# A tuned MLP kernel on one core: pinned casts at the start, and a second level of the recursion in two of the seven products of its second matmul

## The chip, the cores and the metric

One NeuronCore of a Trainium2 chip. The metric is the device time of one launch in microseconds (us), as the median of several executions.

## The reference

The kernel computes a two-layer MLP with a tanh GELU, all inputs and the output in float32.

```python
# x: (8, 1024, 1024)   w1: (1024, 4096)   w2: (4096, 1024)
def reference(x, w1, w2):
    h = x @ w1
    h = 0.5 * h * (1 + np.tanh(np.sqrt(2 / np.pi) * (h + 0.044715 * h ** 3)))
    return (h @ w2).astype(np.float32)
```

## The kernel before

The 8192 rows are worked in eight superblocks of 1024 rows, counted here from 0. In each, a first matmul (with GELU) is followed by a second matmul. Both are cut into 2 by 2 blocks and done with seven products instead of eight (a recursion in the manner of Strassen): sums and differences of blocks are made first, then seven half-size products, then their results are added with signs. Each such phase has 448 matmuls of 512 columns. Only the second matmul of superblock 0 is plain (512 matmuls), because it runs while the second weight is still being loaded, cast to fp16, and summed.

Superblock 0 also stores the cast blocks of the first weight in HBM (`raw_d`) and the summed operands of the second weight (`w2_d`). Superblock 1 reads `raw_d` back and makes the operands of the first weight (`w1_d`), and later superblocks only read. So the start of the program is full of transfers, and the rest is not.

The parts that matter here, cut; `tt` is a `tensor_tensor` on DVE (VectorE), `temp` a 128x512 fp32 tile of a pool of ten, `unit` a 4 KB-per-partition tile of a pool of 26, and `gcp` a pool of four staging tiles:

```python
def cast_in(dst, src, cast):              # fp32 weight from HBM, cast to fp16
    st = gcp.tile([P] + list(dst.shape[1:]), F32, name="gc")   # one of FOUR staging tiles
    load_in_order(st, src)                # SP queue, kept in program order
    cast(out=dst, in_=st)

def store(sb, b, q, src):
    ...
    queue = nc.gpsimd if sb < NSB - 1 else nc.sync
    return queue.dma_start(out=out2[...], in_=src)

def matmul2_first(sb, g, keep_w1):        # superblock 0, plain; b = column half of the weight
    ...
    for b in range(2):
        ...
        for q in range(NI // QC):
            raw = raw_units(QC, OH, (b + 1,))
            for j in range(0, QC, 2):
                for a in range(2):
                    cast_in(..., pool_copy if b == 0 and q < 2 else nc.scalar.copy)
            ...                           # matmuls of these rows of the weight
            if b == 0:
                if q == 0: keep_w1()
                elif q == 1: xb = x_cast(1, pool_last[0])
            else:
                ...                       # sums on DVE, written to w2_d on the SP queue
        if b == 1:
            blocks = x_transpose(xb, load_in_order)
            write(2); write(3)
        for i in range(2 * NQ):           # eight PSUM banks to evict
            ...
            if i % 2: nc.scalar.copy(out=o, in_=banks[i])
            else:     nc.vector.tensor_copy(out=o, in_=banks[i])
            last = store(sb, ..., o)

def matmul2(sb, g):                       # superblocks 1 to 7: seven products
    def product(m, banks, first):
        pieces = [load_ops(d, (m,), QC, OH)[m] for d in w2_d]
        u, v = A_TERMS[m]
        for q in range(NQ):
            if v is None: a = g[u][:, :, cols]
            else:
                a = gcp.tile([P, NI, P], GT, name="gc")
                tt(a, g[u][:, :, cols], g[v][:, :, cols], SUB)
            ...                           # 16 matmuls of 512 columns into banks[q]
            yield q, banks[q]
    ...                                   # products 4, 5, 2, 3
    for q, ps in product(1, rb, True):
        tt(d[q], d[q], ps, ADD)
    for q, ps in product(6, qb, False):
        c22 = temp(); tt(c22, d[q], ps, ADD); store(sb, "22", q, c22)
    for q, ps in product(7, rb, False):
        c11 = temp(); tt(c11, u[q], ps, ADD); last = store(sb, "11", q, c11)
    return last

for sb in range(NSB):
    g, quad = matmul1(xs, sb)
    ...                                   # second matmul
    if sb + 1 < NSB:
        xs = XOps(blocks); xs.make(5, 1, 2, 7, 6)   # five 128x2048 differences of the next x
```

## Time and profile before

| | before |
|---|---|
| time, median of 3 (range) | 1606.53 us (1605.8 to 1607.75) |
| span of the profiled execution | 1603.7 us, mean granted clock 0.996 |
| first matmul of superblock 0 | 18.3 to 130.3 us |
| second matmul of superblock 0 | 130.3 to 245.7 us |
| first matmul of superblock 1 | 245.7 to 342.6 us (96.9) |
| every later phase | 96.69 us |
| last matmul starts / span ends | 1599.4 / 1603.7 us |

Such phase times are read from the trace: a phase runs from the start of its first matmul to the start of the first matmul of the next phase.

Three lines of the page of the kernel before: the span, PE's busy time with its share of the span, and the chain that ended last, by engine.

```profile
span 1603.7 us, 18985 instructions
...
PE 1578.2 (98%) x7296; PEld 717.9 (45%) x7296; DVE 819.6 (51%) x1047; ACT 472.3 (29%) x784; POOL 132.1 (8%) x228
...
PE 95%; DMA 3%; DVE 1%; ACT 1%; issue 0%; SPq 0%; POOL 0%; DVEq 0%
...
```

PE (TensorE) is the limit. The chain of the kernel before, followed in time (start, length, what, how many), shows how regular it is after the start:

```profile
...
245.89 96.87 PE ps L277 x448
342.76 96.69 PE ps L461 x448
...
```

448 matmuls in 96.69 us are 215.8 ns each, with no wait at all. Time can only be saved there by streaming fewer columns. The start is different. The waits of PE of the kernel before (total us, times, longest):

```profile
...
PE ps L277 <- ACT g_216 L287: 7.7, 2, 7.4
...
PE ps L395 <- DVE tmp L443: 3.3, 1, 3.3
...
```

So PE stands once for 7.4 us behind a GELU, which itself stands behind casts on ACT (ScalarE), and once for 3.3 us behind a PSUM eviction on DVE. Both are holes in the start. The cast in front of that GELU was itself waiting for its weight, as the ACT queue of the kernel before shows (start, length, what, and in brackets the idle time before and what ended it):

```profile
...
118.76 1.04 ACT L137 CAST u<-gc 128x1024 f16<-128x1024 f32 x1 [8.00 <-DMA gc<-in_w_dram]
...
```

So the first hole comes from a transfer that is late. Three stretches of the kernel before, of which two are in the start and one reaches into superblock 1 (from and to, length, busy us and instructions of PE, weight load, DVE, ACT, POOL, then the clock, the DMA share, and GB/s):

```profile
...
105.00:115.00 10.00, 10.00 (x49) 4.52 (x47) 4.20 (x7) 5.43 (x8) 2.58 (x6) 1.00 1.04 265
115.00:124.00 9.00, 1.59 (x6) 0.53 (x5) 1.28 (x2) 4.44 (x7) 0.00 (x0) 0.75 0.97 307
232.00:247.00 15.00, 15.00 (x71) 6.76 (x70) 3.84 (x5) 2.55 (x5) 4.42 (x9) 1.00 0.89 349
...
```

In the first two stretches the DMA engines are full (1.04 and 0.97; a share can come out a little over 1), though PE has only 1.59 us of work in the second. In the third PE is busy throughout. The third view of the kernel before is its SP queue, which issues loads and stores in program order (start, time from first to last issue, what, how many):

```profile
...
89.33 44.96 SPq L115 DMA_DIRECT2D gc<-in_w_dram  x20
...
160.05 26.67 SPq L115 DMA_TRANSPOSE u<-xb  x16
...
202.99 4.79 SPq L152 DMA_DIRECT2D u<-raw_d_81  x4
...
```

These are 20 loads of the second weight into the staging tiles, the sixteen transposing loads of the next x, and the first loads of `raw_d` for superblock 1.

### The profile page before, as it was taken

What the parts mean: (1) busy time and instruction counts of PE and PEld (TensorE: products, weight loads), DVE (VectorE), ACT (ScalarE), POOL (GpSimd) and SP (SyncE); (2) the same over time, 40 slices, a digit from 0 to 9 for tenths busy, and PEclk for the clock granted to TensorE, in tenths of its full rate; (3) what the DMA queues carried; (4) which work ended last, traced back from release to release, by engine and by line L of the source; (5) the groups of instructions that cost most, each with busy time, mean ns of one, the idle gap of its engine ahead of it and who ended that gap; (6) DMA issues with size and microseconds to landing.
All of it is one profiled execution on the core that took longest, in us unless ns stands there. A gap on an engine that the chain in (4) does not pass through costs nothing.

```text
span 1603.7 us, 18985 instructions
## 1 busy us (share of the span) xinstructions
PE 1578.2 (98%) x7296; PEld 717.9 (45%) x7296; DVE 819.6 (51%) x1047; ACT 472.3 (29%) x784; POOL 132.1 (8%) x228
## 2 busy tenths in 40 slices
PE   7989999999999999999999999999999999999999
PEld 4434444444444444444444444444444444444444
DVE  6855336644455444555445554456534555455433
ACT  4645104431044210441114410244103431044310
POOL 2230113001100012000120000100001000000000
PEclk9999999999999999999999999999999999999999
DMA  9999998674566646546574565746557464544511
GB/s 306 345 316 361 276 397 280 179 288 146 197 188 184 236 171 228 157 153 262 186 221 144 169 238 197 227 131 226 201 203 246 102 265 158 210 157 178 216 53 53
DMA packets 161820, 338.91 MB, mean 211 GB/s; under 512 B 72257, under 2 KB 78401, under 8 KB 160833
## 3 DMA queue, kind: packets, MB, share of 16 engines
q1 hardware_dynamic: 146944, 278.97, 50.4%
q0 software_dynamic: 14784, 58.73, 11.5%
q8 instruction: 57, 0.93, 0.2%
q14 instruction: 35, 0.28, 0.1%
HBM read 266.34 MB, written 85.98 MB: 220 GB/s over the span
## 4 chain that ended last, share of the span: by engine, by line
PE 95%; DMA 3%; DVE 1%; ACT 1%; issue 0%; SPq 0%; POOL 0%; DVEq 0%
PE ps L277 46%; PE ps L461 42%; PE ps L395 7%; DMA gc<-in_w_dram 2%; DVE u L107 1%; ACT u L137 0%; DVE tmp L107 0%; DMA u<-in_x_dram 0%; DMA u<-xb 0%; SPq L115 0%; POOL u L118 0%; ACT g_218 L287 0%; ACT g_216 L287 0%; ACT g_217 L287 0%; ACT tmp L343 0%
## 5 line engine op out<-in xcount | busy, mean ns | idle before, releaser
L277 PE MATMUL ps<-u 128*128 128x512 f16 x3584 | 779.8, 380 | 13.1 <-ACT g_216 L287 7.7
L107 DVE TENSOR_TENSOR tmp<-tmp,ps 128x512 f32<-128x512 f32 x652 | 447.1, 687 | 661.6 <-PE ps L461 333.3
L277 PEld LDWEIGHTS <-u 128*128 128x128 f16 x3584 | 351.1, 98 | 440.3 <-issue 15.9
L461 PE MATMUL ps<-u,gc 128*128 128x512 f16 x2240 | 485.7, 379 | 0.0
L461 PEld LDWEIGHTS <-gc 128*128 128x128 bf16 x2240 | 219.2, 98 | 264.3
L375 POOL DMA_DIRECT2D out_dram<-tmp x112 | 60.6, 542 | 1108.0 <-ACT tmp L481 733.9
L107 DVE TENSOR_TENSOR u<-u 128x2048 f16<-128x2048 f16 (+2 forms) x110 | 123.0, 1152 | 56.6 <-ACT u L137 21.5
L343 ACT COPY tmp<-ps 128x512 f32<-128x512 f32 x128 | 73.0, 570 | 258.2 <-PE ps L277 258.2
L107 DVE TENSOR_TENSOR tmp<-ps,tmp 128x512 f32<-128x512 f32 x128 | 88.4, 691 | 5.9 <-PE ps L277 1.2
L481 ACT COPY tmp<-ps 128x512 f32<-128x512 f32 x28 | 16.4, 586 | 177.3 <-PE ps L461 177.3
L395 PE MATMUL ps<-u,g_217 128*128 128x512 f16 x128 | 49.0, 383 | 3.3 <-DVE tmp L443 3.3
L395 PE MATMUL ps<-u,g_218 128*128 128x512 f16 x128 | 49.0, 383 | 0.0
L395 PE MATMUL ps<-u,g_215 128*128 128x512 f16 x128 | 48.9, 382 | 0.0
L395 PE MATMUL ps<-u,g_216 128*128 128x512 f16 x128 | 48.8, 381 | 0.0
L137 ACT CAST u<-gc 128x1024 f16<-128x1024 f32 x36 | 37.2, 1044 | 37.6 <-DMA gc<-in_w_dram 37.6
L487 ACT COPY tmp<-ps 128x512 f32<-128x512 f32 x28 | 16.4, 586 | 80.3 <-PE ps L461 80.3
L475 ACT COPY tmp<-ps 128x512 f32<-128x512 f32 x28 | 16.4, 586 | 74.9 <-PE ps L461 74.9
L118 POOL CAST u<-gc 128x1024 f16<-128x1024 f32 (+1 forms) x26 | 28.5, 1105 | 73.8 <-DMA gc<-in_w_dram 60.0
L254 POOL DMA_DIRECT2D xb<-in_x_dram x56 | 27.5, 509 | 18.1 <-DMA out_dram<-tmp 14.5
L441 ACT COPY tmp<-ps 128x512 f32<-128x512 f32 x8 | 4.7, 586 | 71.1 <-PE ps L395 71.1
L395 PEld LDWEIGHTS <-g_218 128*128 128x128 bf16 x128 | 12.6, 98 | 18.8 <-issue 3.9
L395 PEld LDWEIGHTS <-g_215 128*128 128x128 bf16 x128 | 12.6, 99 | 15.5 <-issue 0.8
(120 smaller groups left out, 848.8 us busy)
## 6 DMA issues: line engine op xcount, KB each, us to landing
gc<-in_w_dram SPq DMA_DIRECT2D x64, 512.0 KB, 6.8
out_dram<-tmp POOLq DMA_DIRECT2D x112, 256.0 KB, 4.4
u<-w_d_85 SPq DMA_DIRECT2D x49, 512.0 KB, 6.4
u<-w_d_86 SPq DMA_DIRECT2D x49, 512.0 KB, 7.1
u<-w_d_87 SPq DMA_DIRECT2D x49, 512.0 KB, 5.8
u<-w_d_88 SPq DMA_DIRECT2D x49, 512.0 KB, 6.3
u<-w_d_77 SPq DMA_DIRECT2D x42, 512.0 KB, 4.8
u<-w_d_78 SPq DMA_DIRECT2D x42, 512.0 KB, 5.1
```

What stands on the lines that cost most here:

```text
L107: nc.vector.tensor_tensor(out=out, in0=in0, in1=in1, op=op)
L118: pool_last[0] = nc.gpsimd.tensor_copy(out=out, in_=in_)
L137: cast(out=dst, in_=st)
L254: nc.gpsimd.dma_start(out=xb[q:q + P, :], in_=x2[s * SB + q:s * SB + q + P, :])
L277: nc.tensor.matmul(bank, lhsT=ops[m][:, k, cs], rhs=xs[m][:, k, :], start=(first and k == 0), stop=(k == KH - 1), skip_group_check=not first,)
L343: nc.scalar.copy(out=v, in_=pb)
L375: return queue.dma_start(out=out2[r0:r0 + P, o0:o0 + OH], in_=src)
L395: nc.tensor.matmul(banks[i], lhsT=g[f"{i // NQ + 1}{a + 1}"][:, c, (i % NQ) * P:(i % NQ + 1) * P], rhs=w[a], start=(c == 0 and a == 0), st ...
L461: nc.tensor.matmul(banks[q], lhsT=a[:, c, :], rhs=pieces[c // QC][:, c % QC, :], start=(first and c == 0), stop=(c == NI - 1), skip_group_ ...
L475: nc.scalar.copy(out=v[q], in_=ps)
L481: nc.scalar.copy(out=c21, in_=ps)
L487: nc.scalar.copy(out=c12, in_=ps)
```

## The change

It has three parts. At the start, the casts of the second weight that ACT does are pinned behind the last GELU of the first matmul, some of them go to POOL (GpSimd), and the PSUM evictions go to ACT, to close both holes. From superblock 2 on, products 6 and 7 of the second matmul get a second level of the recursion: instead of 64 matmuls of 512 columns each takes seven small products of 16 matmuls of 256 columns, so 112 x 256 columns in place of 128 x 256, an eighth less. For this superblock 1 splits the operands of these products into `in_d`, and the sums that products 6 and 7 are added to, which were temporaries, become tiles of the pool of 26. And GELU's output is fp16 instead of bf16.

```diff
-GT = mybir.dt.bfloat16
+GT = mybir.dt.float16
+INNER = (6, 7)
+ORDER = (4, 5, 1, 2, 3, 7, 6)
 ...
+    def act_late_copy(out, in_):
+        with tc.issue_after(gelu_last[0].ins):
+            nc.scalar.copy(out=out, in_=in_)
 ...
-            nc.scalar.activation(out=g[b][:, c, :], in_=src, func=GELU)
+            gelu_last[0] = nc.scalar.activation(out=g[b][:, c, :], in_=src, func=GELU)
 ...                                      # matmul2_first
-                            pool_copy if b == 0 and q < 2 else nc.scalar.copy,
+                            pool_copy if (q == 0 if b == 0 else j) else act_late_copy,
 ...
-                    elif q == 1:
+                    elif q == 3:
                         xb = x_cast(1, pool_last[0])
 ...
-                if i % 2:
-                    nc.scalar.copy(out=o, in_=banks[i])
-                else:
-                    nc.vector.tensor_copy(out=o, in_=banks[i])
+                nc.scalar.copy(out=o, in_=banks[i])
 ...
+    def inner_product(m, g, acc):
+        ...                               # seven loads of in_d on the SP queue
+        def outer(b):                     # a block of the product's left operand, made once
+            ...
+                tt(x[b], g[u0][at], g[v0][at], SUB)
+        def product(j, bank, first):
+            u, v = A_TERMS[j]
+            if v is None: t = outer(u)
+            else:
+                p, q = outer(u), outer(v)
+                t = gcp.tile([P, HK, HT // 2], GT, name="gc")
+                tt(t, p, q, SUB)
+            ...                           # 16 matmuls of 256 columns
+        product(4, pb, True)
+        v = temp(); nc.scalar.copy(out=v, in_=pb)
+        product(5, qb, True)
+        u = temp(); tt(u, v, qb, SUB)
+        nc.gpsimd.tensor_tensor(out=part("11"), in0=part("11"), in1=pair(u), op=ADD)
+        ...                               # products 1, 2, 3, 7, 6; one more add on gpsimd
 ...                                      # matmul2
         for q, ps in product(1, rb, True):
             tt(d[q], d[q], ps, ADD)
-        ...                               # products 6 and 7 as above
+            if sb > 1:
+                tt(u[q], u[q], ps, ADD)
+        for m, b, acc2, acc, banks in ((6, "22", d2, d, qb), (7, "11", u2, u, rb)):
+            if sb > 1:
+                inner_product(m, g, acc2)
+                for q in range(NQ):
+                    last = store(sb, b, q, acc[q])
+            else:
+                ...                       # as before
```

More of the change, by code (lines that the diff above doesn't have):

```diff
@@ L94 @@
     raw_d = [dram.tile([P, 4, KH * QW], DT, name=f"raw_d{q}") for q in range(NI // QC)]
+    in_d = {m: dram.tile([P, 7, NI // 2, OH // 2], DT, name=f"in_d{m}") for m in INNER}
     w2_d = [dram.tile([P, 7, QC * OH], DT, name=f"w2_d{q}") for q in range(NI // QC)]
@@ L132, in make_sum @@
         tt(ops[m][:, :, sl], raw[u][:, :, sl], raw[v][:, :, sl], op)
+    def act_late_copy(out, in_):
+        with tc.issue_after(gelu_last[0].ins):
+            nc.scalar.copy(out=out, in_=in_)
+    gelu_last = [None]
     def cast_in(dst, src, cast):
@@ L304, in ahead @@
                 if step == 0:
-                    quads.append(load_ops(w1_d[q], (4, 5, 1, 2, 3, 7, 6), KH, QW))
+                    quads.append(load_ops(w1_d[q], ORDER, KH, QW))
                 return
@@ L439, in matmul2_first, with split_inner, block @@
                 o = temp()
-                if i % 2:
-                    nc.scalar.copy(out=o, in_=banks[i])
-                else:
-                    nc.vector.tensor_copy(out=o, in_=banks[i])
+                nc.scalar.copy(out=o, in_=banks[i])
                 last = store(sb, f"{i // NQ + 1}{b + 1}", i % NQ, o)
         return last, blocks
+    def split_inner(m, pieces):
+        def block(k, b, h):
+            return pieces[2 * k + h][:, :, b * OH // 2:(b + 1) * OH // 2]
+        for j in ORDER:
+            u, op, v = B_TERMS[j]
+            d = in_d[m][:, j - 1]
+            t = None if op is None else unit(NI // 2, OH // 2)
+            for h in range(2):
+                cs = slice(h * QC, (h + 1) * QC)
+                x0 = block(int(u[0]) - 1, int(u[1]) - 1, h)
+                if op is None:
+                    nc.gpsimd.dma_start(out=d[:, cs, :], in_=x0)
+                else:
+                    tt(t[:, cs, :], x0, block(int(v[0]) - 1, int(v[1]) - 1, h), op)
+            if op is not None:
+                nc.gpsimd.dma_start(out=d, in_=t)
@@ new lines, in inner_product, with part, pair @@
+    def inner_product(m, g, acc):
+        HK, HO = NI // 2, OH // 2
+        u0, v0 = A_TERMS[m]
+        x = {}
+        y = {}
+        for j in ORDER:
+            y[j] = unit(HK, HO)
+            nc.sync.dma_start(out=y[j], in_=in_d[m][:, j - 1])
+        def outer(b):
+            if b not in x:
+                a, k = int(b[0]) - 1, int(b[1]) - 1
+                x[b] = unit(HK, HT // 2)
+                at = (slice(None), slice(k * HK, (k + 1) * HK), slice(a * HT // 2, (a + 1) * HT // 2))
+                tt(x[b], g[u0][at], g[v0][at], SUB)
+            return x[b]
+        def product(j, bank, first):
+            u, v = A_TERMS[j]
+            if v is None:
+                t = outer(u)
+            else:
+                p, q = outer(u), outer(v)
+                t = gcp.tile([P, HK, HT // 2], GT, name="gc")
+                tt(t, p, q, SUB)
+            for i in range(2):
+                for c in range(HK):
+                    nc.tensor.matmul(
+                        bank[:, i * HO:(i + 1) * HO],
+                        lhsT=t[:, c, i * P:(i + 1) * P],
+                        rhs=y[j][:, c, :],
+                        start=(first and i == 0 and c == 0),
+                        stop=(c == HK - 1),
+                        skip_group_check=not first or i > 0,
+                    )
+        def part(b):
+            a, o = int(b[0]) - 1, int(b[1]) - 1
+            return acc[a][:, :, o * HO:(o + 1) * HO]
+        def pair(t):
+            return t.rearrange("p (i n) -> p i n", i=2)
+        pb, qb, rb = psum(), psum(), psum()
+        product(4, pb, True)
+        v = temp()
+        nc.scalar.copy(out=v, in_=pb)
+        product(5, qb, True)
+        u = temp()
+        tt(u, v, qb, SUB)
+        nc.gpsimd.tensor_tensor(out=part("11"), in0=part("11"), in1=pair(u), op=ADD)
+        product(1, rb, True)
+        s = temp()
+        tt(s, u, rb, ADD)
+        product(2, pb, False)
+        s2 = temp()
+        tt(s2, s, pb, SUB)
+        nc.gpsimd.tensor_tensor(out=part("22"), in0=part("22"), in1=pair(s2), op=ADD)
+        tt(part("21"), part("21"), pair(pb), ADD)
+        product(3, qb, False)
+        tt(part("12"), part("12"), pair(qb), ADD)
+        product(7, rb, False)
+        tt(part("11"), part("11"), pair(rb), ADD)
+        product(6, qb, False)
+        tt(part("22"), part("22"), pair(qb), ADD)
@@ L469, in product, with halves @@
                 yield q, banks[q]
-        v, u, d, s2 = {}, {}, {}, {}
+            if m in INNER:
+                split_inner(m, pieces)
+        def halves():
+            tiles = [up.tile([P, 2, OH], F32, name="u") for _ in range(2)]
+            return tiles, [tiles[q // 2][:, q % 2, :] for q in range(NQ)]
+        v = {}
         pb, qb, rb = [], [], []
@@ L475, in matmul2 @@
             nc.scalar.copy(out=v[q], in_=ps)
+        u2, u = halves()
         for q, ps in product(5, qb, True):
-            u[q] = temp()
             tt(u[q], v[q], ps, SUB)
+        d2, d = halves()
         for q, ps in product(2, pb, False):
@@ L482, in matmul2 @@
             store(sb, "21", q, c21)
-            d[q] = temp()
             tt(d[q], u[q], ps, SUB)
@@ L488, in matmul2 @@
             store(sb, "12", q, c12)
+            if sb > 1:
+                tt(d[q], d[q], ps, ADD)
         for q, ps in product(1, rb, True):
             tt(d[q], d[q], ps, ADD)
-        for q, ps in product(6, qb, False):
-            c22 = temp()
-            tt(c22, d[q], ps, ADD)
-            store(sb, "22", q, c22)
-        for q, ps in product(7, rb, False):
-            c11 = temp()
-            tt(c11, u[q], ps, ADD)
-            last = store(sb, "11", q, c11)
+            if sb > 1:
+                tt(u[q], u[q], ps, ADD)
+        for m, b, acc2, acc, banks in ((6, "22", d2, d, qb), (7, "11", u2, u, rb)):
+            if sb > 1:
+                inner_product(m, g, acc2)
+                for q in range(NQ):
+                    last = store(sb, b, q, acc[q])
+            else:
+                for q, ps in product(m, banks, False):
+                    c = temp()
+                    tt(c, acc[q], ps, ADD)
+                    last = store(sb, b, q, c)
         return last
```

## The prediction

> **What bounds the kernel now.** TensorE: the page gives PE 98% of the 1603.7 us span, and 95% of the chain that ended last. In order of time that chain shows, from 246 us on, phases (first, then second matmul of superblocks 1 to 7) of 448 matmuls in about 96.7 us each unbroken: 215.8 ns per 512-column matmul, clock 1.00. There only fewer columns can save. The start has two holes, by windows: from 104.6 to 130 us 76 matmuls start (16.4 us of work in 25.4), and from 188 to 196 us 17 (3.7 in 8). Timeline: weight casts ahead of GELUs on ACT wait 8 us for a DMA; a PSUM eviction on DVE sits behind a sum that waits 7.2 us for x transposes. About 13 us are recoverable. DMA is 95% or more busy there, which limits it.
>
> **What the change does.**
> 1. Casts of the second weight are pinned behind the last GELU and shared with POOL; evictions go to ACT. Both holes should close: estimate 11 us. The b=1 casts had 20 us of slack, so they stay hidden.
> 2. In superblocks 2 to 7, products 6 and 7 go from 64 matmuls of 512 columns (13.81 us) to 112 of 256. The Trainium skill's "TensorE: Matmul & The Clock Gate", section "Back-to-back issue gap", gives N/2.4 + 2.5 ns; the trace agrees at 512. At 256 that is 109 ns (estimate), 12.23 us a product: 1.58 us saved, 12 times: 19 us at most. Unshown: that a weight load (98 ns in the groups) hides at 256.
> 3. DVE pays. Before, a product needs 4 subtractions of 128x2048 (1.22 us, 1.15 back to back) and 4 PSUM adds (0.69, 0.62). An inner product needs 9 subtractions and 7 PSUM ops, besides 2 adds on POOL. From product 1 to the end of product 7 DVE has about 40 us of work against 38 of PE. PE runs product 6 nearly free, then waits in product 7 for operands: I estimate 1.3 us per superblock, 2.5 with the POOL adds ("SBUF — State Buffer": the shared port pair is an exclusive lock between GpSimd and DVE ops with two SBUF inputs; not shown by this trace). So 3.16 us saved less 2.5 lost, six times: 4 us net.
> 4. Superblock 1 splits two weights: 20 half-size sums on DVE, 7.3 MB of writes, once: 1 us lost. Operand reads rise by 3.1 MB per later superblock, on 212 GB/s: hidden.
> 5. GELU in fp16: no time.
>
> **Sum.** 1606.5 - 11 - 4 + 1 = 1592 us; 8 in 10: 1579 to 1606. Chances: faster over 2% 0.05, within 2% 0.93, slower 0.02.
>
> **What would show it.** Step 1: superblock 1 starts near 233 us instead of 246; on ACT no cast of the second weight before the last GELU. Step 2: 1344 matmuls of 256 columns, spaced 109 ns where fed. Step 3: PE waits on DVE operands, 1 to 4 us per superblock, in product 7; DVE above 90% busy in the last 38 us of each second matmul, which takes about 96 us. Step 4: phases of superblock 1 within 2 us of 96.7.
>
> **What would make it wrong.** Weight loads not hidden at 256 columns (each 10 ns costs 13 us); POOL adds that block DVE longer, or late weights at the next superblock's start: slower. DVE ahead of my layout: up to 15 us faster. DMA saturation keeping the holes: 10 us slower.

## More of the kernel before

Last, DVE of the kernel before, the first sums of superblock 1 (start, length, what, how many, and in brackets the idle time before and what ended it):

```profile
...
213.41 7.09 DVE L107 TENSOR_TENSOR u<-u 128x2048 f16<-128x2048 f16 x6 [17.25 <-DMA u<-raw_d_81]
...
```

They start 32 us before superblock 1 needs them (213.4 against 245.7).

## The result, and the profile after

The changed kernel took 1621.9 us (median of 4, 1620.85 to 1623.54) against 1607.14 us (1605.8 to 1608.67) for the kernel before on the same chip. The ratio is 1.0092, with a 95% interval of 1.0075 to 1.011. Ratios here and below are the mean time of one kernel's fast runs over that of the other's of the same rounds, so not quite the ratio of the medians. The prediction of 1592 us, with a range up to 1606, was wrong: the change costs 0.9% where a gain of 0.9% was predicted.

| phase, us | before | after | what it adds to the span |
|---|---|---|---|
| first matmul of superblock 1 starts | 245.7 | 232.2 | -13.5 |
| first matmul of superblock 1 | 96.87 | 116.39 | +19.5 |
| second of 1, first of 2 | 96.69 each | 96.69 each | 0 |
| second matmul of superblocks 2 to 6 | 96.69 | 95.52 (69.07 + 26.45) | 5 x -1.17 |
| first matmul that follows it (3 to 7) | 96.69 | 98.21 | 5 x +1.52 |
| second matmul of superblock 7, to the start of the last matmul | 96.5 | 102.0 | +5.5 |
| from the start of the last matmul to the end | 4.4 | 7.1 | +2.7 |

The entries sum to 15.95 us, and the two spans differ by 16.0. 69.07 us are products 4, 5, 2, 3 and 1, which the change leaves alone, and 26.45 us are the two products that it splits (27.62 before).

The page of the kernel after, the same three lines:

```profile
span 1619.7 us, 20521 instructions
...
PE 1568.4 (97%) x7872; PEld 774.0 (48%) x7872; DVE 947.9 (59%) x1203; ACT 481.0 (30%) x800; POOL 188.6 (12%) x274
...
PE 1%; DVE 1%; issue 0%; DVEq 0%
...
```

The chain that ended last now has about 1% of the span in it: it is followed back only over the last part of superblock 7, and is of no use for the rest. The waits of PE of the kernel after answer better:

```profile
...
PE ps L288 <- DVE tmp L111: 21.8, 11, 8.6
PE ps L503 <- DVE gc L111: 8.0, 6, 3.2
...
PE ps L556 <- DMA u<-w_d_87: 2.1, 1, 2.1
...
PE ps L556 <- DMA u<-w_d_90: 0.7, 1, 0.7
...
```

The two holes of the start are gone from the list. In their place PE waits 21.8 us in first matmuls (line 288) for temporaries of DVE, 14.4 of them in superblock 1, 8.0 us in the small products (line 503) for differences of DVE, and 2.8 us in superblock 7 for weight loads. The same stretches of the kernel after:

```profile
...
105.00:115.00 10.00, 10.00 (x48) 4.53 (x47) 6.00 (x9) 4.75 (x8) 0.00 (x0) 1.00 0.56 167
115.00:124.00 9.00, 9.00 (x43) 4.05 (x42) 5.47 (x8) 5.41 (x9) 0.00 (x0) 1.00 0.00 1
232.00:247.00 15.00, 6.17 (x23) 2.45 (x24) 11.55 (x12) 2.34 (x4) 5.89 (x11) 0.74 1.02 395
...
```

From 105 to 124 us PE is now busy throughout, as intended. But the DMA share falls to 0.56 and then to 0.00. And at the start of superblock 1 PE has 6.17 us of work in 15, at a mean clock of 0.74, while the DMA engines are full (1.02, before 0.89). The SP queue of the kernel after, the same three groups:

```profile
...
89.73 58.08 SPq L119 DMA_DIRECT2D gc<-in_w_dram  x20
...
175.74 30.70 SPq L119 DMA_TRANSPOSE u<-xb  x16
...
222.46 3.74 SPq L163 DMA_DIRECT2D u<-raw_d_81  x4
...
```

The 20 weight loads take until 147.8 us instead of 134.3, and all that stands behind them in the queue is later: the transposes by 15.7 us, the loads of `raw_d` by 19.5 us. DVE of the kernel after, at the start of superblock 1:

```profile
...
230.91 2.47 DVE L111 TENSOR_TENSOR u<-u 128x2048 f16<-128x2048 f16 x2 [17.00 <-DMA u<-raw_d_81]
...
245.72 0.69 DVE L111 TENSOR_TENSOR tmp<-tmp,ps 128x512 f32<-128x512 f32 x1 [0.18 <-DMA out_dram<-tmp]
...
250.85 0.69 DVE L111 TENSOR_TENSOR tmp<-tmp,ps 128x512 f32<-128x512 f32 x1 [2.70 <-DMA out_dram<-tmp]
...
```

The first sums of superblock 1 begin at 230.9 us, 17.5 us later than before, and 1.3 us before PE begins the phase. Then DVE waits for stores (`out_dram<-tmp`) to give temporaries back.

Now the second level. Two products of superblock 2 in the kernel before and in the kernel after, by the same stretch (columns as above):

```profile
...
609.00:635.00 26.00, 26.00 (x122) 11.80 (x121) 10.14 (x13) 0.59 (x1) 4.91 (x10) 1.00 0.54 191
...
```

```profile
...
609.00:635.00 26.00, 24.56 (x213) 20.47 (x211) 25.00 (x29) 1.17 (x2) 8.09 (x8) 1.00 0.62 210
...
```

DVE goes from 10.14 us busy to 25.00 of 26. PE of the kernel after in the same place of superblock 3, with its waits in brackets:

```profile
...
813.54 1.91 PE L503 MATMUL ps<-u,gc 128*128 128x256 f16 x16
815.77 1.91 PE L503 MATMUL ps<-u,gc 128*128 128x256 f16 x16 [0.31 <-DVE u L111]
...
820.37 3.67 PE L503 MATMUL ps<-u,gc 128*128 128x256 f16 x32 [0.95 <-DVE gc L111]
...
```

Where PE is fed, small matmuls start 109 ns apart: the 32 of the last line take 3.67 us, the drain of the last one included. In front of them it waits (0.31 and 0.95 us in the brackets) for `u` and `gc`, the operands that DVE makes. The additions on POOL, from the groups of the kernel after (count, busy us, mean ns of one, idle time before and what ended it):

```profile
...
L526 POOL TENSOR_TENSOR u<-u,tmp 128x512 f32<-128x512 f32 x12 | 26.1, 2172 | 279.4 <-DMA u<-in_d_86 223.1 <-DVE tmp L111 56.2
...
L533 POOL TENSOR_TENSOR u<-u,tmp 128x512 f32<-128x512 f32 x12 | 15.2, 1264 | 24.4 <-DVE tmp L111 18.5 <-DMA u<-w_d_77 5.9
...
```

The same addition of 128x512 elements takes 2172 ns in the first place and 1264 in the second; e6 comes back to this.

### The profile page after: what moved, and what is told of

Read it like the earlier page. It is cut to its first block, busy times and chain, and to the rows that moved or that the text cites. A ratio compares the mean times of both kernels' runs of the same rounds, so it can differ in the third digit from the quotient of the medians.

```text
span 1619.7 us, 20521 instructions
## 1 busy us (share of the span) xinstructions
PE 1568.4 (97%) x7872; PEld 774.0 (48%) x7872; DVE 947.9 (59%) x1203; ACT 481.0 (30%) x800; POOL 188.6 (12%) x274
## 5 line engine op out<-in xcount | busy, mean ns | idle before, releaser
L288 PE MATMUL ps<-u 128*128 128x512 f16 x3584 | 785.2, 381 | 26.2 <-DVE tmp L111 21.8
L111 DVE TENSOR_TENSOR tmp<-tmp,ps 128x512 f32<-128x512 f32 x548 | 375.0, 686 | 287.9 <-ACT tmp L354 116.1
L556 PE MATMUL ps<-u,gc 128*128 128x512 f16 x1472 | 320.0, 379 | 0.0
L556 PEld LDWEIGHTS <-gc 128*128 128x128 f16 x1472 | 143.9, 98 | 173.8
L111 DVE TENSOR_TENSOR u<-u,ps 128x512 f32<-128x512 f32 x152 | 101.1, 681 | 98.4 <-ACT tmp L588 66.3
L386 POOL DMA_DIRECT2D out_dram<-tmp x72 | 39.1, 544 | 815.5 <-ACT tmp L583 723.5
L503 PE MATMUL ps<-u,gc 128*128 128x256 f16 x960 | 112.8, 275 | 10.4 <-DVE gc L111 8.0
L354 ACT COPY tmp<-ps 128x512 f32<-128x512 f32 x128 | 73.0, 571 | 117.1 <-PE ps L288 117.1
L503 PEld LDWEIGHTS <-gc 128*128 128x128 f16 x960 | 93.7, 99 | 26.5 <-DVE gc L111 11.6
L111 DVE TENSOR_TENSOR u<-tmp,ps 128x512 f32<-128x512 f32 x28 | 19.3, 688 | 119.0 <-PE ps L556 95.6
L111 DVE TENSOR_TENSOR gc<-u 128x2048 f16<-128x2048 f16 x60 | 74.1, 1267 | 0.0
L583 ACT COPY tmp<-ps 128x512 f32<-128x512 f32 x28 | 16.4, 586 | 177.3 <-PE ps L556 177.3
L526 POOL TENSOR_TENSOR u<-u,tmp 128x512 f32<-128x512 f32 x12 | 26.1, 2172 | 279.4 <-DMA u<-in_d_86 223.1
L522 ACT COPY tmp<-ps 128x512 f32<-128x512 f32 x12 | 7.0, 586 | 162.8 <-PE ps L503 162.8
```

What stands on the lines that cost most here:

```text
L111: nc.vector.tensor_tensor(out=out, in0=in0, in1=in1, op=op)
L288: nc.tensor.matmul(bank, lhsT=ops[m][:, k, cs], rhs=xs[m][:, k, :], start=(first and k == 0), stop=(k == KH - 1), skip_group_check=not first,)
L354: nc.scalar.copy(out=v, in_=pb)
L386: return queue.dma_start(out=out2[r0:r0 + P, o0:o0 + OH], in_=src)
L503: nc.tensor.matmul(bank[:, i * HO:(i + 1) * HO], lhsT=t[:, c, i * P:(i + 1) * P], rhs=y[j][:, c, :], start=(first and i == 0 and c == 0), ...
L522: nc.scalar.copy(out=v, in_=pb)
```

## The experiments

Seventeen kernels ran. All gave the right result except two that were wrong, as said there. This table holds what was measured; "m2" is the second matmul of superblocks 2 to 6 (its two products 6 and 7 alone in brackets), "next m1" the first matmul behind it.

| run | time, us | ratio [95%] | first matmul of superblock 1: start, length | m2 | next m1 |
|---|---|---|---|---|---|
| after | 1621.9 | 1.0092 [1.0075, 1.011] | 232.2, 116.4 | 95.52 (26.45) | 98.21 |
| e1 | 1612.26 | 1.003 [1.0015, 1.0045] | 231.3, 116.5 | 96.69 | 96.69 |
| e3 | 1608.19 | 1.0006 [0.999, 1.0023] | 241.8, 98.3 | 96.69 | 96.69 |
| e4 | 1605.53 | 0.9989 [0.9968, 1.0009] | 232.0, 113.8 | 96.69 | 96.69 |
| e8 | 1608.77 | 1.0012 [0.9997, 1.0027] | 244.4, 102.5 | 96.69 | 96.69 |
| e13 (wrong) | 1594.36 | 0.9924 [0.991, 0.9937] | 234.3, 100.9 | 96.69 | 96.69 |
| e2 | 1618.35 | 1.0068 [1.0052, 1.0083] | 249.9, 97.3 | 95.52 (26.45) | 98.2 |
| e5 (wrong) | 1596.0 | 0.9935 [0.992, 0.995] | 245.4, 97.5 | 93.8 (24.75, once 25.10) | 96.69, once 98.86 |
| e6 | 1616.79 | 1.0064 [1.0048, 1.0079] | 246.2, 97.5 | 96.2 (27.09) | 98.1 |
| e7 | 1606.67 | 1.0003 [0.9986, 1.002] | 244.3, 96.9 | 95.84 (12.96 + 13.81) | 96.69 |
| e11 | 1606.33 | 0.9994 [0.998, 1.0008] | 247.0, 96.9 | 96.69 | 96.69 |
| e9 | 1617.82 | 1.0068 [1.0055, 1.0082] | 245.1, 97.8 | 95.5 (26.45) | 98.2 |
| e10 | 1695.09 | 1.0547 [1.0531, 1.0563] | 248.4, 110.4 | 95.51 (26.45) | 110 to 112 |
| e14 | 1629.18 | 1.0139 [1.0124, 1.0154] | 247.3, 97.4 | 99.0 to 100.2 (29.9 to 31.1) | 96.69 |
| e15 | 1624.56 | 1.0109 [1.0096, 1.0122] | 241.6, 100.6 | 99.0 to 100.1 (29.9 to 31.05) | 96.69 |
| e12 | 1607.4 | 1.0005 [0.9993, 1.0018] | 243.1, 100.0 | 95.84 (12.96 + 13.81) | 96.69 |
| e16 | 1601.87 | 0.9969 [0.9956, 0.9982] | 241.8, 100.7 | 95.84 (12.97 + 13.81) | 96.69 |
| e17 | 1608.69 | 1.0009 [0.9996, 1.0023] | 242.6, 103.1 | 95.07 (26.00, once 26.35) | 96.69 |

The time of the kernel before in these batches was 1606.19 to 1607.74 us. A start of the same instructions varies by some us between executions: superblock 1 begins at 245.7 us in the kernel before and at 249.9 us in e2, which has the same start. So differences of a few us in that column are not read. Behind the first matmul of superblock 1 the phases of e1, e3, e4, e8 and e13 have the same lengths in all traces, so for these five the total times compare the end of that matmul over all executions, and not only in the profiled one.

### The start: e1, e3, e4, e8, e13

My first theory was that the pin starves the DMA engines: casts that wait for the last GELU hold all four staging tiles, so that no weight is loaded meanwhile. The rivals were the second level's extra traffic and the moved evictions.

**e1: the start of the change alone**, on the kernel before.

```diff
 # the kernel before, with act_late_copy and gelu_last as in the change, and
-  pool_copy if b == 0 and q < 2 else nc.scalar.copy,
+  pool_copy if (q == 0 if b == 0 else j) else act_late_copy,
-  elif q == 1:
+  elif q == 3:
       xb = x_cast(1, pool_last[0])
-  if i % 2: nc.scalar.copy(out=o, in_=banks[i])
-  else:     nc.vector.tensor_copy(out=o, in_=banks[i])
+  nc.scalar.copy(out=o, in_=banks[i])
```

> The kernel before with only the changed start: second-weight casts pinned behind the last GELU and shared with POOL, all evictions on ACT, x cast issued at the fourth quarter. Theory A (the start as a whole loses: pinned casts hold the four staging tiles, the SP queue stops issuing loads, every later load is 13 to 18 us later and the next superblock's first matmul waits): superblock 1 starts near 232 us but its first matmul takes about 115 us, total about 6 us slower than before, 1613 us. Rival B (the start gains its 13 us; the loss in superblock 1 comes from the other parts, more rows in the pools and the split of the weights): first matmul of superblock 1 takes 97 us, total 1593 us.

Superblock 1 starts at 231.3 us and its first matmul takes 116.5 us, as in the kernel after. Everything later is 96.69 us. So the loss in superblock 1 belongs to the start, and the second level has no part in it. Stretches of e1:

```profile
...
105.00:115.00 10.00, 10.00 (x48) 4.52 (x47) 5.79 (x9) 4.94 (x9) 0.00 (x0) 1.00 0.46 143
115.00:124.00 9.00, 9.00 (x43) 4.08 (x42) 5.26 (x7) 5.65 (x9) 0.00 (x0) 1.00 0.00 1
...
```

**e3: e1 without the pin.**

```diff
-  pool_copy if (q == 0 if b == 0 else j) else act_late_copy,
+  pool_copy if (q == 0 if b == 0 else j) else nc.scalar.copy,
```

> e1 without the pin alone: casts on the same engines, but where the scheduler puts them. Theory A: loads are issued between 98 and 124 us again, superblock 1's first matmul falls from about 115 to about 97 us, while the hole in front of the last GELUs comes back (about 9 us); eviction on ACT keeps its 4 us: total about 1602 us. Rival C (not the pin but the POOL casts behind output stores, or the earlier x cast, delay the loads): the first matmul of superblock 1 stays above 110 us.

The DMA engines stay busy, the first hole is back, and superblock 1 is no longer slow (98.3 us). The profiled execution is e3's fastest (1602.93 us; the others took 1607.65 to 1608.84), but the other kernels without the pin, e12 and e15 to e17, agree with 100.0 to 103.1 us. Stretches of e3:

```profile
...
105.00:115.00 10.00, 4.80 (x15) 1.84 (x15) 2.69 (x5) 6.56 (x9) 0.00 (x0) 0.83 0.83 266
115.00:124.00 9.00, 8.94 (x42) 3.82 (x41) 4.55 (x8) 8.80 (x14) 0.00 (x0) 1.00 0.96 312
...
```

PE has 13.74 us of work in these 19, against 19.00 in e1, and DMA 0.83 and 0.96 instead of 0.46 and 0.00. The time is that of the kernel before (1.0006). So the pin does both: it closes the hole and starves the transfers. Up to 124 us the rates and lengths of two stretches (0 to 124 and 124 to 232 us, not printed) give 35.7 MB moved with the pin (288 GB/s times 124 us, in e1 and after), 39.7 MB in e3, and 40.2 MB before. At 232 us it is 69.3 MB after and 76.8 MB before.

**e4: POOL does all casts of the first half** and ACT only few of the second.

```diff
-  pool_copy if (q == 0 if b == 0 else j) else act_late_copy,
+  pool_copy if (b == 0 or j) else act_late_copy,
```

> e1 with all casts of the first half of the second weight on POOL, which waits for no GELU; the pin stays for the second half. Theory A: staging tiles come free at once, no DMA hole at 105 to 124 us, superblock 1 starts near 232 us and its first matmul takes 97 to 102 us: total 1593 to 1598 us. Rival D (DMA bandwidth itself bounds the start, whatever the order): the first matmul of superblock 1 ends no earlier than in before, 342 us, total 1605 us or more.

Now nothing waits for GELU in the first half, the transfers keep up (40.1 MB at 124 us), and the hole is closed: superblock 1 begins at 232.0 us. Yet its first matmul takes 113.8 us, and it ends at 345.8, no earlier than before (342.6). So starvation is not the whole story: over all executions e4, which has none, is 6.6 us faster than e1 (means), and yet no faster than the kernel before (0.9989 [0.9968, 1.0009]). The profiled execution is e4's slowest (1608.68 us; the others took 1602.4 to 1606.4), so its end at 345.8 is some us later than usual. The trace of e4 shows two waits there, 5.1 us behind sums that wait for a `raw_d` load, and 8.0 us for temporaries held by stores. Between 232 and 262 us its DMA share is 1.03 and 1.05 (shown below, beside e13).

**e8: e4 with the output stores of superblock 0 on ACT's queue.**

```diff
-  queue = nc.gpsimd if sb < NSB - 1 else nc.sync
+  queue = nc.scalar if sb == 0 else nc.gpsimd if sb < NSB - 1 else nc.sync
```

> e4 with superblock 0's output stores issued from the ACT queue instead of POOL's, where they stand behind weight stores that wait for DMA. If the 8.5 us stall at 242 us (DVE waits for a free temporary, that is for such a store) is POOL's queue order: it goes, superblock 1's first matmul falls from 113.8 to about 105 us, total 1597 us. Rival D (DMA is saturated there, so the wait only moves): it stays above 110 us.

This missed. ACT evicts PSUM and now also waits to issue stores, so that PE waits 7.6 us for evictions in the second matmul of superblock 0, and superblock 1 begins at 244.4 us. Its first matmul is shorter (102.5 us) but ends at 346.8, much as in e4 (345.8). Moving the wait to another queue does not remove it.

**e13: e4 with 6.3 MB less to write.** Three of the four writes of `raw_d` are left out and all loads read the one that is written, so the result is wrong; the bytes read stay the same.

```diff
-  for b, t in self.raw.items():
+  for b, t in self.raw.items() if self.q == 0 else ():        # keep_raw
-  nc.sync.dma_start(out=flat(t), in_=raw_d[q][...])
+  nc.sync.dma_start(out=flat(t), in_=raw_d[0][...])
```

> e4 with three of the four raw copies of the first weight not written (superblock 1 reads the first copy four times; result wrong on purpose): 6.3 MB less DMA before 140 us, nothing else. In e4 the PE hole is closed and yet superblock 1's first matmul ends at 345.8 us. Theory D (from 124 us the start is bound by DMA throughput of about 400 GB/s): loads run earlier by up to 16 us, superblock 1's first matmul falls from 113.8 to 97 to 104 us and ends at 329 to 337 us; total 1590 to 1598 us. Rival I (bytes do not matter, the order of queues does): it ends after 342 us again.

The first matmul of superblock 1 takes 100.9 us instead of 113.8, and ends at 335.2 us, 10.6 us earlier than in e4. Stretches of e4, then of e13:

```profile
...
232.00:247.00 15.00, 5.47 (x21) 2.12 (x20) 1.88 (x3) 2.37 (x4) 4.82 (x9) 0.71 1.03 419
247.00:262.00 15.00, 11.38 (x43) 4.64 (x43) 5.61 (x9) 4.14 (x7) 6.61 (x13) 0.72 1.05 315
...
```

```profile
...
232.00:247.00 15.00, 11.10 (x53) 4.93 (x51) 5.36 (x7) 4.57 (x8) 8.99 (x18) 1.00 1.01 356
247.00:262.00 15.00, 15.00 (x71) 6.77 (x70) 10.85 (x15) 7.46 (x13) 1.73 (x4) 1.00 0.77 187
...
```

In e4 the DMA engines are full in both, and PE has 5.47 and 11.38 us of work in 15. In e13 the share is down to 0.77 in the second, and PE is busy there. So fewer bytes make superblock 1 earlier, where closing the holes did not: at full DMA, an earlier first use does not make data come earlier, and closing the holes alone moves the wait to superblock 1. One rival stays open: e13 takes the twelve writes out of the SP queue too, and superblock 1 no longer waits for them before it reads, so bytes and queue are not told apart. That another queue did not help in e8 fits the Trainium skill, "DMA: Bandwidth & Descriptors", section "Issuing engines are not separate DMA queues", which says that transfers of all issuing engines end up on the same 16 DMA engines; the full share in e4, with stores on one queue and loads on another, is in line with it.

### The second level: e2, e5, e6, e7, e11

**e2: the second level alone**, with the start of the kernel before.

```diff
 # the kernel after, with
-  pool_copy if (q == 0 if b == 0 else j) else act_late_copy,
+  pool_copy if b == 0 and q < 2 else nc.scalar.copy,
-  elif q == 3:
+  elif q == 1:
       xb = x_cast(1, pool_last[0])
-  nc.scalar.copy(out=o, in_=banks[i])
+  if i % 2: nc.scalar.copy(out=o, in_=banks[i])
+  else:     nc.vector.tensor_copy(out=o, in_=banks[i])
```

> The changed kernel with the start of before (casts, evictions, x cast as before). Theory A: the second level costs about 10 us by itself (0.35 us in each of superblocks 2 to 6, 5.4 us in superblock 7, 2.9 us in the tail), so about 1617 us, and the first matmul of superblock 1 takes 97 us. Rival B: that matmul still takes over 110 us and the total is above 1625 us.

It costs 0.7% by itself. Its phases repeat those of the kernel after: 26.45 us instead of 27.62, then 98.2 instead of 96.69, superblock 7 at 101.7, and 7.0 us after the last matmul.

**e5: e2 without the inner differences** (wrong): the small products use a block itself.

```diff
-  p, q = outer(u), outer(v)
-  t = gcp.tile([P, HK, HT // 2], GT, name="gc")
-  tt(t, p, q, SUB)
+  t = outer(u)
+  outer(v)
```

> e2 with the five operand subtractions of each small product left out (result wrong on purpose; all matmuls, loads and PSUM work stay): 11.5 us of DVE work less per second matmul. Theory A (DVE's queue is what PE waits for): the fourteen small products take 24.5 us instead of 26.45, the next first matmul 96.7 instead of 98.2, superblock 7's small products about 24.5 instead of 29.8; total about 1600 us. Rival E (256-column matmuls or the operand loads are the limit): the small products stay at 26 us or more.

The two products take 24.75 us, and the next first matmul 96.69 (in one superblock each, 25.10 and 98.86). Stretches of e5, from the start of two split products to the end of the next first matmul:

```profile
...
799.00:826.00 27.00, 26.51 (x232) 22.36 (x230) 20.94 (x26) 1.76 (x3) 11.70 (x14) 1.00 0.66 239
826.00:923.00 97.00, 97.00 (x451) 44.01 (x450) 56.56 (x82) 46.35 (x79) 3.42 (x8) 1.00 0.70 234
...
```

224 matmuls at 109.2 ns are 24.46 us (worked out), so weight loads do hide at 256 columns, and 2.87 of the 3.16 us per superblock are gained (27.62 before) when DVE has five differences less to make per product. The formula in the Trainium skill, "TensorE: Matmul & The Clock Gate", section "Back-to-back issue gap" (109 ns at 256), holds. So what superblocks 2 to 6 lose is lost to DVE's five differences per product. Two losses stay in e5: products 4, 5, 2, 3 and 1 of superblock 7 still take 72.95 us instead of 69.07, and the end still takes 7.0 us (both are taken up under e9).

**e6: e2 with the two additions per product moved from POOL to DVE.**

```diff
-  nc.gpsimd.tensor_tensor(out=part("11"), in0=part("11"), in1=pair(u), op=ADD)
+  tt(part("11"), part("11"), pair(u), ADD)
   # and the same for part("22")
```

> e2 with the four POOL adds per superblock on DVE. Theory A with a small lock: DVE gets 2.4 us more and loses about 2 us of lock waits, so small products 26 to 27.5 us, next first matmul 98 to 99 us, total within 8 us of e2. Rival F (the POOL adds, which take 2.2 us and stretch DVE subtractions to 1.7 us and more, are the main loss): small products fall below 25.5 us and the total by 6 us or more.

27.09 and 98.1 us, against 26.45 and 98.2 in e2. The wait of PE for differences grows from 8.0 us in e2 to this in e6:

```profile
...
PE ps L506 <- DVE gc L111: 13.2, 11, 3.2
...
```

The POOL additions and DVE's differences do hold each other up. In superblock 3 of the kernel after, an addition that starts 0.17 us into a difference takes 2.17 us instead of 1.26, and a difference that starts 0.43 us into an addition takes 1.92 us instead of 1.22. So whichever starts first keeps the other waiting. This agrees with the exclusive lock described in the Trainium skill, "SBUF — State Buffer", section "SBUF: two separate sides", which the trace of the kernel before could not show. But the same additions done on DVE cost as much, so moving them gains nothing in the products; what the lock costs by itself was not measured. The end does change: 4.9 us pass after the last matmul, against 7.0 in e2 (see e9).

**e7: only product 6 at the second level.**

```diff
-INNER = (6, 7)
+INNER = (6,)
   # and without the addition of product 1 to u
```

> e2 with the second level in product 6 alone, product 7 as before. Theory A: DVE has a whole normal product to catch up, so product 6 costs 12.3 to 12.7 us, the next first matmul 96.7: superblocks 2 to 7 gain 1.1 to 1.5 us each; total 1600 to 1606 us, 12 to 18 below e2. If the second level loses in itself, whatever DVE does, it is half of e2's loss: about 1612 us.

Product 6 takes 12.96 us (12.23 would be without waits, 13.81 before), product 7 its 13.81, and the next first matmul 96.69: a gain of 0.85 us in each of five superblocks. Superblock 7 gives it back (100.5 us; PE waits for weight loads behind stores), and the time is that of before, 1.0003.

**e11: fp16 for GELU's output alone.**

```diff
-GT = mybir.dt.bfloat16
+GT = mybir.dt.float16
```

> The kernel before with GELU's output in fp16 alone. All theories: within 3 us of before (the start varies by that), every phase after superblock 0 at 96.69 us, weight load 98 ns, GELU 630 and 597 ns.

All phases take 96.69 us and the ratio is 0.9994. It costs nothing.

### Where things stand in the queues: e9, e10, e14, e15

**e9: e2 with all stores on POOL's queue**, in the last superblock too.

```diff
-  queue = nc.gpsimd if sb < NSB - 1 else nc.sync
+  queue = nc.gpsimd
```

> e2 with the last superblock's output stores on POOL's queue like all others, instead of SP's. Theory A for superblock 7 (stores that wait for results stand in SP's queue ahead of weight loads; and the scheduler, having other queues to fill, orders DVE there unlike elsewhere): its second matmul takes 95.5 us as in superblocks 2 to 6 instead of 101.7, total 4 to 7 us below e2's 1618. Rival G (superblock 7 is slow because no next x and weights are loaded, so something else is late): it stays at 100 us or more.

The second matmul of superblock 7 falls from 101.7 us to 95.4 (69.07 + 26.34), like the others. So its loss came from stores that stood ahead of weight loads in the SP queue, which also changed the order in which the scheduler (which orders each engine's queue when the program is built) put DVE's work. But the end is lost again: the last stores of e9 on POOL are issued here, and the span ends at 1613.9 us.

```profile
...
1601.67 1.07 POOL L386 DMA_DIRECT2D out_dram<-u  x2 [0.76 <-DVE u L111]
```

From the last matmul to the end it takes 13.6 us, against 7.0 in e2. The total does not move.

It is not the landing of these stores that takes so long: their last packet is there at 1604.5 us. What ends last is a `DRAIN` that closes POOL's queue. Its groups in e9, in the kernel after, and in e16 (below), in this order (line, queue, how many; shortest, median and longest in ns; first and last start):

```profile
...
L651 POOLq DRAIN  x3: 46/93/11010, 1602.1 to 1613.6; - x3
...
```

```profile
...
L648 POOLq DRAIN  x3: 46/102/10377, 1608.5 to 1619.4; - x3
...
```

```profile
...
L646 POOLq DRAIN  x3: 46/93/8646, 1582.5 to 1598.3; - x3
...
```

The first and longest of them starts with POOL's last instruction and takes 11.0 us in e9, 10.4 us in the kernel after. In all nine traces with about 7 us or more after the last matmul (after, e2, e5, e9, e10, e12, e14, e15, e17) the span ends 0.8 us after it, and it ends 8.3 to 10.4 us after POOL's last instruction. In the other ten (4.2 to 4.9 us) POOL was done early and the `DRAIN` was over before the last stores landed, as in e16, where it ends at 1591.2 us. So the end of these nine hangs on when POOL gets its last instruction, be it a store (e9, e12) or one of the second level's additions (the other seven). Why it takes so long, no run shows.

**e10: e2 with the five x differences made ahead of the second matmul.** In e2 they stand in DVE's queue at the start of the next first matmul.

```diff
+  xs = XOps(blocks); xs.make(5, 1, 2, 7, 6)     # moved ahead of
   last = matmul2(sb, g)
```

> e2 with the five sums of the next superblock's x written ahead of the second matmul instead of after it, so that they do not stand in DVE's queue between the last small product and the next first matmul. Theory A: the first matmuls of superblocks 3 to 7 fall from 98.2 to about 96.8 us, the small products stay near 26.4; total 6 to 8 us below e2. Rival H (the first matmul is late for its weights): 98.2 us stays.

This missed badly: the first matmuls of superblocks 1 to 6 take 110 to 112 us. In the DVE queue the differences now stand ahead of work of the first matmul, and wait up to 14.0 us for transposes; behind the longer waits the matmuls also start 427 instead of 216 ns apart for some us. Waits of PE of e10:

```profile
...
PE ps L288 <- DVE tmp L111: 60.7, 9, 12.3
...
```

(The rows of this view are total, times, longest.) Superblock 7 has no next x, and its first matmul takes 96.69 us. That the x differences cause the 1.5 us is thereby made likely; e14 shows it.

**e14: e2 with the x differences between products 3 and 1.**

```diff
   for q, ps in product(3, qb, False):
       ...
+  xs = XOps(blocks); xs.make(5, 1, 2, 7, 6)
   for q, ps in product(1, rb, True):
```

> e2 with the five sums of the next x between products 3 and 1, where DVE has room and the x blocks have landed (e10 put them too early, in front of the transposes). Theory A: first matmuls of superblocks 3 to 7 take 96.7 us instead of 98.2; small products 26 to 27 us; total 6 to 8 us below e2. If the first matmul waits for something else, 98.2 stays.

The next first matmul is 96.69 us in every superblock: the 1.5 us were the x differences. But the two products grow from 26.45 to 29.9 or more. Waits of PE of e14:

```profile
...
PE ps L506 <- DVE gc L111: 19.3, 6, 3.2
...
```

The scheduler now puts all four blocks of product 7 ahead of its first difference, and PE waits 3.2 us once per superblock. It is the order that superblock 7 has in the kernel after and in e2.

**e15: the kernel after without the pin, with the x differences as in e14, and with a changed queue for stores.**

```diff
+  pool_copy if (q == 0 if b == 0 else j) else nc.scalar.copy,
+  queue = nc.gpsimd if sb < NSB - 1 or b != "11" else nc.sync
   # and e14's edit
```

> A version meant to beat both kernels: changed kernel without the pin, x sums as in e14, the last superblock's stores on POOL except its last product's on SP (e9's tail was 13.6 us with all on POOL). Second matmuls 95.5, first ones 96.7, start as before or 3 us better, tail about 6 us: 1597 to 1602 us.

This missed: it is the same as e14, first matmuls at 96.69, products at 29.9 to 31.05. In superblock 7 they take 26.34, as in e9, since most stores are off the SP queue.

**e17: both products, with DVE's order from product 1 to product 7 laid down by hand.** The operands of product 6 are made during product 1, and those of product 7 between the additions of product 6.

```diff
+  def ptt(out, in0, in1, op):
+      tc.keep_in_program_order(nc.vector.tensor_tensor(out=out, in0=in0, in1=in1, op=op))
   # used for all DVE work of these products, in an order written out; else as e15
```

> Both products at the second level, first casts not pinned, x sums made between products 3 and 1 as in e14 and e15, but the order of the vector engine's queue from product 1 to product 7 is laid down by hand: operands of product 6 are made during product 1, those of product 7 between product 6's additions, and no operand stands behind another that waits. My theory (the small products lose to the order of the vector queue, not to the matmuls): small products 24.5 to 25.5 us in superblocks 2 to 7 instead of 26.45 (no laid order) or 29.9 (e14, e15), next first matmul 96.7, so about 17 us less than before in these six superblocks; total 1586 to 1597 us, faster than e16's 1601.9. Rival (the vector engine or its contention with the additions on GpSimd is the limit, whatever the order): small products 26.5 us or more, or the waits move into product 1 or the next superblock, and the total is no better than 1600 us.

The products take 26.00 us and the next first matmul 96.69, so together 1.62 us less than before per superblock. It is more than any other order gave, and short of the 24.5 to 25.5 that I expected. Stretches of e17:

```profile
...
599.00:633.00 34.00, 32.96 (x258) 24.82 (x256) 33.38 (x38) 1.17 (x2) 8.90 (x8) 1.00 0.69 243
...
```

From 599 to 633 us DVE is busy 33.38 of 34 us. So the order accounted for part of the loss, and here the engine itself is the limit: both theories hold in part. The total is no better than before, as superblock 7 takes 97.7 us (one wait of 2.7 us at 1553 us), the first matmul of superblock 1 takes 103.1, and 9.3 us pass after the last matmul, as in e15: POOL's last addition ends at 1594.3 us, its `DRAIN` at 1604.4, 4.6 us after the SP queue with the last stores is done (1599.8). What e17 takes with POOL done earlier was not run.

### Together: e12, e16

**e12: no pin, product 6 only, all stores on POOL.**

```diff
+  pool_copy if (q == 0 if b == 0 else j) else nc.scalar.copy,
+INNER = (6,)                            # and without the addition of product 1 to u
+  queue = nc.gpsimd
```

> Changed kernel with the pin taken away, the second level in product 6 alone, all stores on POOL's queue: first matmul of superblock 1 about 97 us, second matmuls 95.8 us in superblocks 2 to 7, start as in e3. Theory A: 1597 to 1602 us, 5 to 10 below before.

The phases are as hoped (superblock 7 takes 95.9 us), and 11 us after the last matmul take it all back: 1.0005. POOL's `DRAIN` ends at 1605.4 us there, and the last stores have landed at 1598.5.

**e16: e12, with the last stores on the SP queue again.**

```diff
-  queue = nc.gpsimd
+  queue = nc.gpsimd if sb < NSB - 1 or b != "11" else nc.sync
```

> e12 with the last product's stores on SP instead of POOL: e12's tail of 11 us falls to about 4 to 5 us, all phases as in e12 (second matmuls 95.8): 1599 to 1604 us.

1601.87 us, ratio 0.9969 [0.9956, 0.9982]: faster than both kernels, by 0.3% against the kernel before. 4.2 us pass after the last matmul, as POOL has nothing to do after 1583.2 us, and superblock 7 keeps 95.9 us. What is left of waits for DVE in its small products, over all six superblocks:

```profile
...
PE ps L503 <- DVE u L111: 3.1, 5, 0.8
...
```

## Why the prediction was wrong

- **Step 1, the start: the step that failed.** The prediction said "Both holes should close: estimate 11 us. The b=1 casts had 20 us of slack, so they stay hidden." The holes closed, and superblock 1 begins at 232.2 us where 233 was predicted. But 19.5 us come back in its first matmul. e1 shows that this is the start's doing, and e3 that it goes when the pin goes, while the hole comes back: with the pin, staging tiles held by casts that wait for the last GELU let the DMA share fall to 0.00 for 9 us. What had slack was the casts. The loads, sums and writes that stand behind them in one queue had none. e4 and e13 show the deeper fault: with the starvation gone and the holes closed, superblock 1 is still 17 us slow, and 6.3 MB fewer bytes make it 10.6 us faster. The start is limited by transfers, as far as e13 can tell bytes from queue order. The prediction came near this ("DMA saturation keeping the holes"), but only as a chance that the holes stay, worth 10 us; they closed, and the wait moved.
- **Step 2, the gain per product: right.** 109 ns a matmul where fed, weight loads hidden; e5 has 24.75 us for two products against 24.46 in theory.
- **Step 3, DVE's price: the second step that failed.** It was right in kind, but counted only inside the products and not behind them. The 2.5 us predicted inside the products were about 2.0 us (26.45 against 24.46). Not foreseen were 1.5 us in the next first matmul, because the x differences find DVE late (shown by e14), and in superblock 7 an extra 5.5 us, from stores ahead of weight loads in one queue and the order of DVE's work that followed (e9). The end of the program grew by 2.7 us, of which 2.1 are POOL's `DRAIN` behind its last additions (it ends at 1618.9 us, the SP queue with the stores at 1616.8); e6, with these additions on DVE, has 2.1 us less of it than e2. So "4 us net" gained became about 10 us lost (+1.75, +5.5 and +2.7).
- **Step 4, the splits in superblock 1: its test failed, its cost did not exist.** The second matmul of superblock 1, where the splitting is done, takes 96.69 us. The first is 19.7 us beyond 96.7, for the reason of step 1.
- **Step 5, fp16: right** (e11).
- The sum was -11 - 4 + 1 = -14 us in the prediction. It was -13.5 + 19.5 for the start and +10 for the second level, +16 in the profiles.

Open: why POOL's `DRAIN` takes 8 us and more, whether e13's gain comes from the bytes or from the shorter queue, and how much of the few us by which starts differ between executions is in each single start.

## What to carry to other kernels

A hole in PE during a stretch where the DMA engines are full is not free time: ask what the transfers do if the hole closes, and look at the DMA share again afterwards, above all where casts hold staging tiles that loads need. A saving on the bottleneck that is paid in work of another engine has to be costed up to the point where that engine is idle again, including the next phase and the last one. The last instruction that an engine gets can set the end of the program, as POOL's did here. And the order in which a queue holds its work can be worth as much as the work: here the same two products took 26.0, 26.45 or 29.9 us by what stood ahead of what on DVE, so splitting one product of two gave what splitting both did not.

## What the Trainium skill lacked or had wrong

- "TensorE: Matmul & The Clock Gate", section "Back-to-back issue gap", calls N/2.4 + 2.5 ns the gap of an isolated matmul and gives about 131 ns per matmul at 512 columns as sustained in a stream of weight loads and matmuls. In this case such a stream runs at 215.8 ns for 448 matmuls on end, with every weight loaded anew, and at 109 ns with 256 columns: the formula holds for streams, and the 131 ns are not seen.
- The same page, Part 1, is borne out: after a wait of 8.8 us in superblock 1 the matmuls of the kernel after start 427 ns apart for 4.6 us, then 216 ns (the page has 426.7 and 215.7). A wait for data thus costs more than its length. The wait of 2.7 us in e17 is not followed by slow matmuls.
- "SBUF — State Buffer", section "SBUF: two separate sides", has the lock between DVE and GpSimd as it shows here, but not the durations of such work: an addition of 128x512 on GpSimd goes from 1.26 to 2.17 us behind it, a difference of 128x2048 on DVE from 1.22 to 1.92. Each is held up by a little less than what was left of the other (0.91 of 1.05 us, 0.70 of 0.83).
- No page that I read warns that work pinned on one engine can starve the transfers through the staging tiles that it holds (DMA share 0.00 for 9 us, and 4.5 MB fewer moved by 124 us), nor that the `DRAIN` that closes POOL's queue takes 8.3 to 11.9 us (all 19 traces) and sets the end of a program that gives POOL work late (13.6 us after the last matmul in e9, 4.2 in e16).
